# A two-layer hybrid trunk: the mixers' later modulation sums moved from VectorE to TensorE

## The chip, the cores and the metric

One core of one Trainium2 chip runs the whole program. The metric is the device time of one execution in microseconds (us). Three timed runs of the kernel before are shown; the profile is of one further execution. The core's engines work side by side, each through its own queue in order: TensorE (PE: matmuls into PSUM, with PEld for its weight loads), VectorE (DVE), ScalarE (ACT), GpSimd (POOL), and SyncE (SP), which here issues the DMA transfers.

## The reference, cut to what matters

```python
for l in range(DEPTH):                        # 2 layers
    mod = silu(c) @ ada_w[l] + ada_b[l]       # c: 1024 numbers, ada_w[l]: 1024 x 6144
    sh_m, sc_m, g_m, sh_f, sc_f, g_f = split(mod, 6)
    h = rms_norm(x, norm_mix[l]) * (1 + sc_m) + sh_m      # x: 256 x 1024
    proj = h @ w_in[l]
    y_rw, y_ssd, y_fox = three causal mixers on parts of proj
    merged = sum of sigmoid(gate) * (y @ projection)
    x = x + g_m * (merged @ w_out[l])
    h = rms_norm(x, norm_ffn[l]) * (1 + sc_f) + sh_f
    f = dense SwiGLU (l = 0) or top-2-of-8 experts (l = 1)
    x = x + g_f * f
```

The change concerns `mod`, a product of one vector of 1024 numbers and a matrix of 1024 x 6144 in each layer, in float32.

## The kernel before, in words

**Modulations.** A layer's `mod` has six parts of 1024 columns, and each part two halves of 512: 12 halves a layer, 24 in all, each a sum over 1024 rows of `ada_w`. The rows are cut into eight row tiles of 128 x 512, and `silc` holds silu(c) as a column of 128 for each row tile.

The first four halves (scale and shift of the first mixer) are made at the start by `first_half` (L245): eight matmuls whose stationary operand is one column of `silc` broadcast to 32, so that each uses a quarter of TensorE's columns and writes 32 of the 128 PSUM partitions; row tiles 0 to 3 go to quarters 0 to 3, and tiles 4 to 7 are added to them. ACT copies the bank to SBUF with the factor 1/32, and four matmuls of one column with `ones` then sum over partitions and turn the half into columns.

The other 20 halves wait in `mod_queue` and are taken one by one by `mod_next` (L290). Eleven are made during the mixers (layer 0: four, then two; layer 1: four, then one), nine in the first layer's FFN. `mod_load` (L196) issues their transfers on SP:
- where `deep` is not set, four transfers of two row tiles each into `araw`, which has two buffers, so that the third and the fourth transfer wait until the sum has read the first and the second;
- where it is set, eight transfers of one row tile each into the ring `u` of 15 buffers. The sum is then made at the next call.

`mod_sum` (L216) makes the sum on VectorE: one multiply (L220) and seven multiply-adds (L222) of 128 x 512, in the mixers into a tile of the ring `u`, in the FFN into `macc`. `mod_finish` (L225) later turns the result into columns as above.

**The mixers.** Weights come in pieces `raw` of 128 x 2048, are split by ACT (`hi`, L151) and VectorE (`lo`, L152) into two parts, and go through three TensorE products each (`mm3`, L119), with the activations `hh` and `hl` or with a mixer's result. Projections gather in PSUM banks `pd` and `ps` (two buffers each), and the recurrent mixer, the FoX mixer and the modulations use `pm` (four buffers). The recurrent mixer (`rwkv_half`, L525) is a chain of small matmuls, masks (L660, L694) and copies, with matmuls of 32 columns among them.

**Order.** The steps of the mixers are written out by hand in `ORDER`: each word is one step of a generator, and `mo` and `md` are the calls of `mod_next` (the second is the deep one). The framework's scheduler then orders each engine's queue by the order of the program and by its own estimate of when operands are ready; that order is fixed at compile time, so an engine that waits for one instruction's operand holds the rest of its queue. `issue_after` and `behind` put an instruction's queue place behind another's on the same engine. `copied` (L1486, used at L1502) is the copy of the last of the first four halves; ACT's norm work of the column tiles 2 to 7 is placed behind it in both layers.

Of the kernel before, what the change touches and what calls it, by code (L numbers as in the profile page):

```python
# [14 lines left out]
AF = mybir.ActivationFunctionType  # L15
# [4 lines left out]
P = 128  # L20
T = 256
D = 1024
KD = D // P
# [14 lines left out]
NUNIT, NSSD, NSPLIT, NRAW, NB8 = 15, 7, 5, 3, 4  # L38
# [19 lines left out]
def trunk(  # L58
# [5 lines left out]
    pe, act, dve, pool = nc.tensor, nc.scalar, nc.vector, nc.gpsimd  # L64
# [7 lines left out]
    def nm(s):  # L72
        serial[0] += 1
        return f"{s}_{serial[0]}"
# [5 lines left out]
    def const(name, shape, dtype=F32):  # L80
        return cst.tile(shape, dtype, name=name, tag=name)
# [7 lines left out]
    def dbank():  # L89
        return psum.tile([P, 512], F32, name=nm("pd"), tag="pd", bufs=2)  # L90

    def mbank():
        return psum.tile([P, 512], F32, name=nm("pm"), tag="pm", bufs=4)

    def sbank():
        return psum.tile([P, 512], F32, name=nm("ps"), tag="ps", bufs=2)
# [19 lines left out]
    def mm(o, lhsT, rhs, start=True, stop=True):  # L116
        pe.matmul(o, lhsT, rhs, start=start, stop=stop)  # L117
# [49 lines left out]
    def unit(mx, a, b, dtype=F32):  # L167
        return mx("u", [P, a, b], dtype, bufs=NUNIT)
# [10 lines left out]
    silc = const("silc", [P, KD])  # L179
# [8 lines left out]
    def mod_put(l, part, half, ps):  # L188
        o = part * 8 + half * 4
        return dve.tensor_tensor(mods[l][part][:, half * 4:half * 4 + 4], ps, adab[l][:, o:o + 4], op=ALU.add)  # L190
# [3 lines left out]
    mark = {}  # L194
# [19 lines left out]
            mod_sum(sc, raws, key)  # L214

    def mod_sum(sc, raws, key):  # L216
        for kt, raw in enumerate(raws):
            if kt == 0:
                acc = sc("u", [P, 512], bufs=NUNIT) if sc is mx else sc("macc", [P, 512], bufs=3)
                dve.tensor_scalar_mul(acc, raw, silc[:, kt:kt + 1])  # L220
            else:
                dve.scalar_tensor_tensor(acc, raw, silc[:, kt:kt + 1], acc, op0=ALU.mult, op1=ALU.add)  # L222
        mod_late.append((acc, *key))
# [11 lines left out]
    mx = Scope("mix0", stack)  # L235
    FIRST = [(p, h) for p in (1, 0) for h in range(2)]
    araws, last_raw = [], []

    def first_load(n):
# [2 lines left out]
        last_raw.append(nc.sync.dma_start(raw, rows(ada_w[0], (n % 2) * 512, 512, p * D + h * 512, 512)))  # L242
        araws.append(raw)

    def first_half(n):  # L245
        ps = sbank()
        for kg in range(2):
            for q in range(4):
                mm(ps[32 * q:32 * q + 32, :], silc[:, 4 * kg + q:4 * kg + q + 1].broadcast_to([P, 32]), araws[2 * n + kg][:, q, :], kg == 0, kg == 1)
        acc = mx("u", [P, 512], bufs=NUNIT)  # L250
        copied = act.activation(acc, ps, AF.Copy, scale=1.0 / 32)
        ps = dbank()
        for j in range(4):
            mm(ps[:, j:j + 1], acc[:, j * P:(j + 1) * P], ones[:, 0:1])
        mod_put(0, *FIRST[n], ps[:, 0:4])
        return copied

    def make_params(l):
        pp = pcol[:, PCOL + l * NCOL:PCOL + (l + 1) * NCOL]
# [68 lines left out]
    def norm_rows(scr=None, route=False, pieces=4):  # L328

        s8, ss, rs = small(2 * pieces), small(2), small(2)  # L330
        w = D // pieces
        for q in range(pieces):
            for t in range(2):
                if t * w % 512 == 0:
                    sq = sbank()
                o = t * w % 512
                squared = act.activation(sq[:, o:o + w], xr[:, t, q * w:q * w + w], AF.Square, accum_out=s8[:, pieces * t + q:pieces * t + q + 1])
        dve.tensor_reduce(ss, s8.rearrange("p (t q) -> p t q", t=2), AX, ALU.add)
        meant = dve.tensor_scalar(ss, ss, 1.0 / D, EPS, op0=ALU.mult, op1=ALU.add)
        last = rsq(rs, ss)  # L340
        mark.update(root=last, mean=meant, square=squared)
        xt = []
        for k2 in range(KD // 2):
            ps = mbank()
            for k in range(2):
                for t in range(2):
                    transpose(ps[:, k * T + t * P:k * T + (t + 1) * P], xr[:, t, (2 * k2 + k) * P:(2 * k2 + k + 1) * P])
                xt.append(ps[:, k * T:(k + 1) * T])
        if route:
            return xt, rs, last  # L350
        rb = sbank()[:, :T]
        for t in range(2):
            mm(rb[:, t * P:(t + 1) * P], rs[:, t:t + 1].broadcast_to([P, P]), ident)
        rbs = scr()[:, :T]
        act.activation(rbs, rb, AF.Copy)
        return xt, rbs, rs, last

    @contextlib.contextmanager
    def behind(*names):

        with ExitStack() as es:
            for n in names:
                es.enter_context(tc.issue_after(mark[n].ins))
            yield
# [1093 lines left out]
    for lv in range(6):  # L1458
# [8 lines left out]
        ps = mbank()  # L1467
# [15 lines left out]
    first_half(1)  # L1483
    first_half(2)
    normed = norm_rows(lambda: unit(mx, 1, 512)[:, 0, :])
    copied = first_half(3)  # L1486
    last_load = last_raw[7]
    with tc.issue_after(last_raw[7].ins):
        prow = const("prow", [P, 2, 56])
# [3 lines left out]
    for l in range(2):  # L1493
        if l > 0:
            stack = ExitStack()
            mx = Scope("mix1", stack)
        with stack:
            if l > 0:
                normed = norm_rows(lambda: unit(mx, 1, 512)[:, 0, :], pieces=2)
            aff = mod_affine(l, 1, 0, prm["pp"][:, NMIX:NMIX + 8])  # L1500
            norm_cols(aff, normed, 0, 2)
            with tc.issue_after(copied.ins):  # L1502
                norm_cols(aff, normed, 2, KD)
            dump(f"hh{l}", hh)
            run, made = {}, {"y": [None] * 3}
            done = object()

            def part(step):

                i = int(step[1]) if step[1:] in tuple("0123") else 0  # L1510
                if step == "G":
                    made["merged"] = mx("b8", [P, KD, T], bufs=NB8)
                    return gates(mx, l, prm, 0, made["merged"])
                if step[0] == "m":
                    return merge(mx, l, prm, i, made["merged"], made["y"][i], (proj_rw, proj_ssd, proj_fox)[i][l], (4, 8, 4)[i], i == 0)
                return made[step[0]](i)

            def take(step):

                if step == "sc":  # L1520
                    made["key"] = unit(mx, 2, T)
                    made["gl"] = first_cols(l, mx, prm, made["key"])
                    made["r"] = lambda i: rwkv_half(mx, l, prm, made, i)
                elif step == "dt":
                    made["dt"] = logits(mx, made["gl"])
                elif step == "rw":
                    made["y"][0], made["rwkv"] = rwkv(mx, l, prm, lora, made["gl"])
                elif step == "sd":
                    made["y"][1], made["s"] = ssd(mx, l, prm, made["dt"])
                elif step == "fx":  # L1530
                    made["y"][2], made["f"] = fox(mx, l, prm, made["dt"])
                elif step == "mo":
                    mod_next(mx, 0)
                elif step == "md":
                    mod_next(mx, MOD_LEFT[l], True)
                elif step == "gm":
                    while mod_late and mod_late[0][2] == 2:
                        mod_finish(mbank)
                    gm = keep("vfirst", [P, 2, 512]) if l == 1 else mx("u2", [P, 2, 512])
                    made["gm"] = [gm[:, 0], gm[:, 1]]  # L1540
                    mod_row(lambda: unit(mx, 4, P), l, 2, 0.5, made["gm"])
                else:
                    if step not in run:
                        run[step] = part(step)
                    assert run[step] is not None, step
                    if next(run[step], done) is done:
                        run[step] = None
                    return
                assert step in ("mo", "md") or run.setdefault(step, None) is None, step

            with behind("root"):
                take("sc")
            with behind("root"), tc.issue_after(last_load.ins):
                for word in ORDER[l].split()[1:]:
                    name, _, n = word.partition("*")
                    for _ in range(int(n or 1)):
                        take(name)
            assert all(next(g, done) is done for g in run.values() if g)
            merged, gm = made["merged"], made["gm"]
            dump(f"merged{l}", merged)  # L1560
            hh, hl = pair("hh", "hl")
            mod_flush(mx)
            for j in range(0, KD, 2):
                split(merged[:, j:j + 2, :], hh[:, j:j + 2, :], hl[:, j:j + 2, :])
            if l == 0:
                project_out(l, gm, hh, hl)
# [90 lines left out]
```

## Time and profile before

| | us |
|---|---|
| median of three runs | 2163.5 (2162.01 to 2163.97) |
| the profiled execution | 2159.08 |
| its span, first to last instruction | 2157.4 |
| TensorE (PE) busy in the span | 2062.7 |
| VectorE (DVE) busy | 1802.5 |
| ScalarE (ACT) busy | 1383.4 |

The first layer's mixers reach from the start to about 490 us, its FFN from there to about 690, the second layer's mixers to about 1140, and its experts to the end. In the rows below a line number such as L117 is one of the kernel; where a helper issues an operation, as L117 does for all matmuls, the tiles tell them apart: `pd<-hh,hi` writes `pd` from `hh` and `hi`. A count of matmul records is larger than that of the program's instructions where an fp32 product is done in two passes. The chain of waits follows the work that ended last back through the program; its shares say which engine's work, or which transfer, the end waited for.

### The profile page before, as it was taken

The numbers are of one execution on the slowest core, as the hardware profiler recorded it, in microseconds if no ns is written. First come the engines' busy times: TensorE is split into PE (matmuls) and PEld (weight loads), VectorE is DVE, ScalarE is ACT, GpSimd is POOL, SyncE is SP. The second block draws the span as 40 slices with busy tenths as digits, with TensorE's granted clock in tenths as the row PEclk, the third lists the DMA queues.
The fourth block names the chain that finished last, engine by engine and source line by source line (L and its number), as shares of the span: only waits on it lengthen the run. The fifth ranks groups of instructions, "written<-read, shape, count | busy, mean of one in ns | idle before, by whom it ended". The sixth has DMA issues, their size and how long they took to land.

```text
span 2157.4 us, 35317 instructions
## 1 busy us (share of the span) xinstructions
PE 2062.7 (96%) x13291; PEld 1792.2 (83%) x13291; DVE 1802.5 (84%) x2827; ACT 1383.4 (64%) x2198; POOL 146.0 (7%) x184
## 2 busy tenths in 40 slices
PE   6889999999999889999998999999999999999998
PEld 4768799999998878889997888888888887888776
DVE  5877976768776898877678999998999989998887
ACT  3544565555444636556557787878778777877775
POOL 2032300000001032220000000000000000000000
PEclk8999999999999989999999999999999999999999
DMA  8522456557885534426478999999999999999994
GB/s 297 160 75 59 133 183 195 183 181 261 294 281 167 156 100 136 118 87 205 150 230 297 347 371 346 344 353 380 359 331 367 364 356 353 340 343 372 341 354 169
DMA packets 314770, 546.77 MB, mean 253 GB/s; under 512 B 10752, under 2 KB 141952, under 8 KB 314592
## 3 DMA queue, kind: packets, MB, share of 16 engines
q1 hardware_dynamic: 314592, 544.44, 73.2%
q8 instruction: 106, 1.74, 0.3%
q14 instruction: 72, 0.59, 0.1%
HBM read 543.36 MB, written 1.05 MB: 252 GB/s over the span
## 4 chain that ended last, share of the span: by engine, by line
PE 71%; DVE 13%; issue 12%; DMA 2%; ACT 1%; POOL 0%; SPq 0%; DVEq 0%; ACTq 0%; POOLq 0%
PE pd L117 36%; PE pm L117 28%; DVE lo L152 6%; PE ps L117 5%; PE pm L126 1%; DVE u L707 1%; PE ps L126 1%; DVE cu L872 1%; DMA araw<-in_ada_w_dram 1%; DVE xr L1381 1%; DMA prow<-in_heads_dram 1%; ACT hi L151 1%; DVE u L222 0%; DVE dcol L277 0%; DVE lo L433 0%
## 5 line engine op out<-in xcount | busy, mean ns | idle before, releaser
L151 ACT ACTIVATE hi<-raw 128x1024 fp32r<-128x1024 f32 (+2 forms) x1200 | 1026.5, 872 | 507.9 <-PE pd L117 300.4
L152 DVE TENSOR_TENSOR lo<-raw,hi 128x1024 fp32r<-128x1024 f32 (+2 forms) x1200 | 1158.4, 994 | 175.7 <-ACT hi L151 149.7
L117 PE MATMUL pd<-hh,hi 128*128 128x256 f32 (+1 forms) x1184 | 348.6, 296 | 15.9 <-DVE gl L478 3.6
L117 PE MATMUL pd<-hl,hi 128*128 128x256 f32 (+1 forms) x1184 | 342.7, 290 | 0.0
L117 PE MATMUL pd<-hh,lo 128*128 128x256 f32 (+1 forms) x1184 | 342.3, 290 | 0.0
L117 PE MATMUL pm<-lo,hh 128*128 128x512 f32 x672 | 264.8, 395 | 4.5 <-DVE lo L152 4.2
L117 PE MATMUL pm<-hi,hh 128*128 128x512 f32 x672 | 264.6, 394 | 1.1 <-ACT a L1336 1.1
L117 PE MATMUL pm<-hi,hl 128*128 128x512 f32 x672 | 262.0, 390 | 0.0
L117 PEld LDWEIGHTS pd<-hh,hi 128*128 128x128 f32 (+1 forms) x1184 | 232.3, 197 | 28.7 <-issue 10.0
L117 PEld LDWEIGHTS pd<-hl,hi 128*128 128x128 f32 (+1 forms) x1184 | 232.7, 197 | 3.1 <-issue 2.7
L117 PEld LDWEIGHTS pd<-hh,lo 128*128 128x128 f32 (+1 forms) x1184 | 232.2, 196 | 1.8 <-issue 1.2
L117 PE MATMUL pd<-lo,hi 128*128 128x512 f32 x448 | 174.7, 390 | 0.0
L117 PE MATMUL pd<-hi,hi 128*128 128x512 f32 x448 | 170.3, 390 | 0.1
L117 PE MATMUL pd<-hi,lo 128*128 128x512 f32 x448 | 168.2, 390 | 0.0
L117 PEld LDWEIGHTS pm<-lo,hh 128*128 128x128 f32 x672 | 126.2, 188 | 34.9 <-DVE lo L152 9.5
L117 PEld LDWEIGHTS pm<-hi,hh 128*128 128x128 f32 x672 | 126.2, 188 | 28.8 <-ACT a L1336 1.5
L117 PEld LDWEIGHTS pm<-hi,hl 128*128 128x128 f32 x672 | 126.2, 188 | 25.3
L117 PE MATMUL pm<-hi,more 128*128 128x512 f32 x448 | 141.8, 392 | 0.0
L117 PEld LDWEIGHTS pd<-hi,lo 128*128 128x128 f32 x448 | 84.1, 188 | 18.0 <-DVE lo L152 0.2
L117 PEld LDWEIGHTS pd<-hi,hi 128*128 128x128 f32 x448 | 84.1, 188 | 17.9 <-ACT hi L432 0.5
L117 PEld LDWEIGHTS pm<-hi,more 128*128 128x128 f32 x448 | 84.1, 188 | 17.5 <-ACT hi L151 0.3
L117 PEld LDWEIGHTS pd<-lo,hi 128*128 128x128 f32 x448 | 84.1, 188 | 17.3
(436 smaller groups left out, 3394.7 us busy)
## 6 DMA issues: line engine op xcount, KB each, us to landing
raw<-in_moe_w_gu_dram SPq DMA_DIRECT2D x224, 1024.0 KB, 7.0
raw<-in_moe_w_down_dram SPq DMA_DIRECT2D x110, 1024.0 KB, 7.0
raw<-in_w_in_dram SPq DMA_DIRECT2D x66, 1024.0 KB, 5.5
araw<-in_ada_w_dram SPq DMA_DIRECT2D x68, 512.0 KB, 4.9
raw<-in_ffn_w_gu_dram SPq DMA_DIRECT2D x22, 1024.0 KB, 6.6
raw<-in_ffn_w_down_dram SPq DMA_DIRECT2D x11, 1024.0 KB, 6.5
raw<-in_w_in_dram SPq DMA_DIRECT2D x16, 512.0 KB, 5.3
raw<-in_proj_ssd_dram SPq DMA_DIRECT2D x8, 1024.0 KB, 5.7
```

The source lines that it names most:

```text
L117: pe.matmul(o, lhsT, rhs, start=start, stop=stop)
L126: pe.transpose(o, i, ident[:n, :n])
L151: act.activation(hi, raw, AF.Copy)
L152: dve.tensor_sub(lo, raw, hi.bitcast(F32))
L707: dve.transpose(blk(bds[ch], q)[:, odd, bcol(q)], by4(blk(pz, q))[:, odd, :])
L872: dve.scalar_tensor_tensor(cu[:, s:T], ps[:, 0:T - s], pph[:, w:w + 1], cu[:, s:T], op0=ALU.mult, op1=ALU.add)
L1381: dve.tensor_add(xr[:, t, hs], xr[:, t, hs], po)
```

## The change

In the mixers `mod_sum` calls a new function, `quarter_sums`, which makes the sum on TensorE in a `pm` bank, as the first four halves are made in an `ps` bank, and lets ACT copy it into a tile of `u`. The FFN's nine halves stay on VectorE. `first_half` calls the same function. `copied` is no longer handed back; the copy is kept in `mark`, so that in the second layer the place behind it is that of the latest such copy traced.

```diff
     def mod_sum(sc, raws, key):
-        for kt, raw in enumerate(raws):
+        if sc is mx:
+            acc = quarter_sums(mbank(), raws)
+        for kt, raw in enumerate(raws if sc is not mx else ()):
             if kt == 0:
-                acc = sc("u", [P, 512], bufs=NUNIT) if sc is mx else sc("macc", [P, 512], bufs=3)
+                acc = sc("macc", [P, 512], bufs=3)
                 dve.tensor_scalar_mul(acc, raw, silc[:, kt:kt + 1])
             else:
                 dve.scalar_tensor_tensor(acc, raw, silc[:, kt:kt + 1], acc, op0=ALU.mult, op1=ALU.add)
...
+    def quarter_sums(ps, raws):
+
+        for kt in range(KD):
+            q = slice(32 * (kt % 4), 32 * (kt % 4) + 32)
+            mm(ps[q, :], silc[:, kt:kt + 1].broadcast_to([P, 32]), raws[kt], kt < 4, kt >= 4)
+        acc = mx("u", [P, 512], bufs=NUNIT)
+        mark["copied"] = act.activation(acc, ps, AF.Copy, scale=1.0 / 32)
+        return acc
+
     def first_half(n):
-        ps = sbank()
-        for kg in range(2):
-            for q in range(4):
-                mm(ps[32 * q:32 * q + 32, :], silc[:, 4 * kg + q:4 * kg + q + 1].broadcast_to([P, 32]), araws[2 * n + kg][:, q, :], kg == 0, kg == 1)
-        acc = mx("u", [P, 512], bufs=NUNIT)
-        copied = act.activation(acc, ps, AF.Copy, scale=1.0 / 32)
+        acc = quarter_sums(sbank(), [araws[2 * n + kt // 4][:, kt % 4, :] for kt in range(KD)])
         ps = dbank()
         for j in range(4):
             mm(ps[:, j:j + 1], acc[:, j * P:(j + 1) * P], ones[:, 0:1])
         mod_put(0, *FIRST[n], ps[:, 0:4])
-        return copied
...
-            with tc.issue_after(copied.ins):
+            with behind("copied"):
                 norm_cols(aff, normed, 2, KD)
```

## Rows read from the trace of the kernel before

**Rows 1.** The page: busy time, share of the span and instructions of each engine.

```profile
PE 2062.7 (96%) x13291; PEld 1792.2 (83%) x13291; DVE 1802.5 (84%) x2827; ACT 1383.4 (64%) x2198; POOL 146.0 (7%) x184
```

**Rows 2.** Chain of waits by line: 40-100, 250-340, 340-480, 760-860, 960-1060, 1060-1140 us.

```profile
by line: PE pd L117 44.7%; DMA araw<-in_ada_w_dram 11.6%; DVE lo L152 8.0%; DVE cu L872 4.8%; issue 4.5%; ACT hi L151 4.3%; DVE u L222 3.6%; PE pm L117 3.3%; DVE u L605 1.2%; DVE u L615 1.1%; DVE u L616 1.1%; DVE u L606 1.0%; DVE u L609 1.0
by line: PE pd L117 58.2%; PE pm L117 20.3%; PE ps L117 15.5%; PE pm L126 5.4%; PE ps L126 0.6%; issue 0.1%
by line: PE pd L117 78.8%; PE ps L117 11.6%; PE pm L117 7.4%; PE pm L126 2.5%
by line: PE pd L117 27.4%; PE pm L117 11.2%; DMA araw<-in_ada_w_dram 8.9%; DVE lo L152 8.6%; issue 8.3%; DVE u L222 6.2%; DVE u L707 5.2%; PE ps L117 4.3%; DVE s L920 3.2%; DVE b L660 3.1%; PE pm L126 2.7%; DVE cu L872 1.7%; POOL sm L129 1.
by line: PE pd L117 66.8%; PE ps L117 14.4%; PE pm L117 10.9%; PE pm L126 5.4%; ACT hi L151 0.7%; issue 0.6%; ACT b L432 0.6%; ACT u L1015 0.4%; ACT u L1014 0.4%
by line: PE pd L117 78.7%; PE ps L117 14.8%; PE pm L117 4.1%; PE pm L126 2.6%
```

**Rows 3.** Instructions on `silc`: ns min/median/max, first and last start us, forms.

```profile
L222 DVE SCALAR_TENSOR_TENSOR u<-araw,silc,u x56: 732/746/754, 56.2 to 1024.2; 128x512 f32<-128x512 f32 x56
...
L222 DVE SCALAR_TENSOR_TENSOR u<-u,silc,u x21: 740/747/754, 379.3 to 1056.9; 128x512 f32<-128x512 f32 x21
...
L220 DVE TENSOR_SCALAR u<-araw,silc x8: 477/478/484, 55.1 to 1011.4; 128x512 f32<-128x512 f32 x8
L220 DVE TENSOR_SCALAR u<-u,silc x3: 481/482/485, 378.8 to 1046.0; 128x512 f32<-128x512 f32 x3
```

**Rows 4.** First instructions of sums (L220) by stretch: length, VectorE busy (count), clock, DMA.

```profile
40.00:100.00 60.00, 0.48 (x1) 0.96 0.59 176
250.00:480.00 230.00, 2.15 (x5) 1.00 0.60 188
750.00:860.00 110.00, 0.97 (x2) 0.94 0.41 125
950.00:1060.00 110.00, 1.44 (x3) 1.00 0.54 172
```

**Rows 5.** TensorE in order of time, the last of the first four halves.

```profile
28.50 1.06 PE L117 MATMUL ps<-b,silc 128*32 128x512 f32 x8
29.38 1.04 PE L117 MATMUL ps<-raw,silc 128*32 128x512 f32 x8
```

**Rows 6.** TensorE in order of time, around 32-column matmuls of the recurrent mixer.

```profile
142.75 0.28 PE L117 MATMUL pd<-hl,hi 128*128 128x256 f32 x1
142.87 0.28 PE L117 MATMUL pd<-hh,lo 128*128 128x256 f32 x1
143.08 0.64 PE L117 MATMUL pm<-u,c 128*32 128x128 f32 x16
143.65 0.39 PE L117 MATMUL pd<-hh,hi 128*128 128x256 f32 x1
```

**Rows 7.** Waits of the whole span: us in total, times, longest.

```profile
DVE u L222 <- DMA araw<-in_ada_w_dram: 7.0, 9, 1.6
```

**Rows 8.** DMA issues: KB each, median us from issue to landing.

```profile
araw<-in_ada_w_dram SPq DMA_DIRECT2D x68, 512.0 KB, 4.9
```

**Rows 9.** Stretches: length, busy PE, PEld, DVE, ACT, POOL (instructions), clock, DMA.

```profile
55.15:69.20 14.05, 12.64 (x103) 12.38 (x103) 12.45 (x35) 7.70 (x17) 0.00 (x0) 1.00 0.92 274
249.75:266.19 16.44, 16.32 (x150) 14.62 (x149) 16.13 (x34) 11.63 (x33) 3.40 (x2) 1.00 0.53 166
288.12:301.21 13.09, 13.09 (x105) 12.86 (x106) 12.04 (x27) 8.27 (x20) 1.79 (x2) 1.00 0.97 324
750.00:786.00 36.00, 27.42 (x203) 20.96 (x202) 34.13 (x60) 12.41 (x33) 15.17 (x13) 0.87 0.47 137
841.00:857.00 16.00, 15.50 (x118) 13.93 (x117) 14.29 (x31) 7.54 (x17) 5.83 (x5) 1.00 0.68 215
```

**Rows 10.** Instructions of L251, the copy out of PSUM: ns min/median/max.

```profile
L251 ACT ACTIVATE u<-ps x4: 575/588/597, 11.3 to 37.9; 128x512 f32<-128x512 f32 x4
```

**Rows 11.** TensorE's waits in 40 to 250 us: us in total, times, longest.

```profile
PE pm L117 <- DVE u L707: 3.7, 5, 1.3
```

**Rows 12.** The DMA queue's waits in 0 to 490 us: us in total, times, longest.

```profile
SPq L207 <- DVE u L222: 27.5, 12, 8.3
```

More of the change, by code (lines that the diff above doesn't have):

```diff
@@ L1485, in trunk @@
     normed = norm_rows(lambda: unit(mx, 1, 512)[:, 0, :])
-    copied = first_half(3)
+    first_half(3)
     last_load = last_raw[7]
```

## The prediction, made before the change was run

> **What bounds the kernel now.** I read the page's busy shares first, then the chain of waits stretch by stretch, then the rows of the sums themselves. TensorE is busy 96% of the span and VectorE 84% [rows 1]; as averages these decide nothing, so the question is which engine ends last where the sums stand. The chain of waits answers it [rows 2]. In 250 to 480 us, in 960 to 1060 us and after, practically all of it lies on TensorE lines: whatever TensorE gets there makes the kernel longer, and whatever VectorE loses there gives nothing back. In 40 to 100 us and in 760 to 860 us it is mixed: VectorE lines stand in it, among them the sums themselves with the transfers that they wait for ("DMA araw" and "DVE u L222"): 11.6% and 3.6% of 60 us, 8.9% and 6.2% of 100 us, 24.2 us in all.
>
> Eleven of the twenty later modulations are summed in the mixers: the eight first instructions on `araw` and the three on `u` [rows 3]. By stretches, one starts in 40 to 100 us, five in 250 to 480, two in 750 to 860, three in 950 to 1060 [rows 4]. So eight of eleven stand where the chain is all TensorE, and three where VectorE is on it. In the order of the program the mixer of the first layer has four of a first kind (`araw`: two transfers ahead, two asked for during the sum) and then two of a deep kind (`u`: all eight transfers a step ahead), the second layer's four and one. So the eight on the all-TensorE stretches are five of the first kind and three deep ones, and the three on the mixed stretches are of the first kind.
>
> **What goes.** Per modulation one multiply of 0.478 us and seven multiply-adds of 0.746 us [rows 3], 5.70 us of VectorE; 62.7 us for eleven.
>
> **What comes on TensorE.** Eight fp32 matmuls of 32 columns against 128x512, recorded as two passes each. Four of them run at once: in the first four modulations the eight records of one group start within 0.03 us, and the next group starts 0.88 us later, two passes of 0.44 us [rows 5]. What a block of such matmuls costs among full-width ones is seen in the recurrent mixer's 32-column groups: between full-width matmuls 0.12 us apart, a block of 16 records holds the next back until 0.78 us after the last [rows 6]. Less 0.12 and four waves of 128 columns (0.44/4 = 0.11 each) that leaves 0.22 us for changing into column tiles and back. So:
> - a deep modulation, all eight together: 4 x 0.44 + 0.22 = 1.98 us;
> - one of the first kind in two blocks of four: 2 x (0.88 + 0.22) = 2.20 us; in three blocks (four, then two and two, because the third and the fourth transfer land apart): 3.30 us. I take 2.20, because the 32-column groups of the row stand together in TensorE's order and both late transfers can be asked for after one block of 0.9 us; 3.30 stays in the range.
>
> The Trainium skill ("TensorE: Matmul & The Clock Gate", Part 3, measured speedup) gives 3.07 times for four tiles, not four. By that a pass of four would be 0.57 us instead of 0.44, and the eight modulations below would cost 4.2 us more; the next wave's start in the row decides for 0.44.
>
> Where the chain is all TensorE this adds 5 x 2.20 + 3 x 1.98 = 16.9 us, and no row of the chain there shows anything that it could hide behind. If the cover in the other three is missing, they add 2.20 each.
>
> **A wait that moves.** VectorE now waits for `araw` transfers, 7.0 us in 9 times over the eight modulations of the first kind [rows 7], 0.88 us each. A transfer takes 4.9 us from issue to landing in the middle [rows 8]. On VectorE that wait held up `lo` splits, which mostly had room; on TensorE every matmul behind it stands, and so does the next split that waits for its buffers. Bounds for the five: nothing (TensorE has other work ahead of them) to 4.4 us (the same wait). I take half, 2.2.
>
> **What the three on the mixed stretches give back.** Here the engine that is late next is TensorE.
> - 55.15 to 69.20 us: VectorE busy 12.45 of 14.05, TensorE 12.64 [rows 9]. At best the 5.70 of sums and the 1.6 of idle go, 7.3. But TensorE's 12.64 + 2.20 is 14.84, 0.8 more than the stretch. Between +7.3 and -0.8 I take the middle, 3.3.
> - 750 to 786 us: VectorE busy 34.13 of 36.00, TensorE 27.42 [rows 9]. Bounds 0 and 6.4 (36.00 - 27.42 - 2.20). VectorE is 95% busy, so I take 5.0.
> - 841 to 857 us: VectorE 14.29, TensorE 15.50 of 16.00 [rows 9]; 15.50 + 2.20 is 1.7 too long, and VectorE's part is 5.7 at best. Middle: 2.0.
>
> Together 10.3 us.
>
> **Edits at no cost.** The copy out of PSUM, 0.59 us [rows 10], is new on ACT eleven times; ACT is busy 7.7 of 14.05, 8.27 of 13.09 and 11.63 of 16.44 us beside the sums [rows 9], so its idle time hides it; without that cover the eight would add 4.7 us. The sum now holds one of the four `pm` banks from its first matmul to the copy, beside the recurrent mixer, whose matmuls wait at most 1.3 us for the last of their banks' readers [rows 11]; no row shows three banks instead of four; 0 to 3.9 us for the three mixed places, and I take 0. More of the ring `u` stays free, and SyncE's queue, which waits 27.5 us for the sums in the first mixer [rows 12], with weight loads behind it, is let go earlier; I take nothing, because no transfer stands in the all-TensorE chain. The marker for ACT's later norm work is the old one in the first layer, and in the second an instruction long done: 0. The first four modulations issue what they did, and all transfers stay the same in number, size and queue: 0.
>
> **Sum.** 16.9 + 2.2 - 10.3 = +8.8 us. The profiled execution took 2159.08 us (span 2157.4, 1.7 around it); 4.4 below the median of the runs, 2163.5. The sum on its own time is 2167.9; on the median 2172.3. A difference under 0.2%, 4.3 us, can't be told from none here.
>
> **Rivals.**
> - *VectorE's relief decides (faster).* At the three mixed places all 24.2 us of sums and their transfers leave the chain, and the new blocks fall into TensorE's waits there. Then 16.9 - 24.2 = -7.3: 2156.2. For it: VectorE is 95% busy at 750 to 786 us, and SyncE's queue stands behind the sums. Against it: in that stretch other VectorE work runs beside the transfer wait (it idles 1.9 of 36 us), and at 841 us TensorE is as full. It decides once more than 21.2 us leave the chain.
> - *Both cancel (same).* Two thirds of the 24.2 us go, 16.1, and TensorE waits for no transfer: +0.8, 2164.3.
> - *TensorE stands for the late half each time (much slower).* If the second half follows the first at once in TensorE's order, each of the five waits a whole 4.9 us transfer: 24.5 instead of 2.2, +31.1, 2194.6. For it: VectorE's waits for `araw` show that the order runs ahead of the transfers. Against: they are 0.8 us, not 4.9. The Trainium skill ("TensorE: Matmul & The Clock Gate", Part 2, step by step) says that matmuls keep their program order and only weight loads are drawn ahead; by that nothing behind such a wait could pass it.
> - *The tiles don't run together.* If other matmuls are put between the four, each costs 0.88 + 0.22: 8.8 instead of about 2.1 us, eight times: +53.6 on the forecast, 2226. Against it: the groups that stand together [rows 5, 6].
>
> **How the numbers follow.** Forecast 0.46; relief decides 0.22; both cancel 0.24; whole transfer waits 0.05; tiles apart 0.03. Faster 0.22, same 0.24, slower 0.46 + 0.05 + 0.03 = 0.54. The forecast's own range goes from 2167 (waits nothing, a little more given back) to 2186 (three blocks each, 5.5 more; the whole wait, 2.2 more; some 6 of the give-back or of a bank missing). The range takes in the faster case: 2156 to 2186, and leaves out the last two rivals and half of the far ends.
>
> **What would show it.** In the profile after: VectorE's busy time 62 us lower; 176 new fp32 records of 32 columns on `pm`, whose groups of eight start 0.88 us apart; TensorE's chain still whole in 250 to 480 us and that mixer's tail some 11 to 14 us longer from 250 us on; the recurrent stretch at 750 to 786 us about 5 us shorter; small TensorE gaps before the second halves, ended by "DMA araw". Wrong if TensorE's chain at 250 to 480 us turns out to have room for the blocks, or if the two early stretches shorten by over 20 us together.

## The result, and the profile after

The median of three runs is 2224.05 us (2223.91 to 2225.54) against 2163.5, a ratio of 1.0281 [1.0267, 1.0294]: 60.6 us slower. The forecast was 2172 us, 2156 to 2186. The sign was right and the size wrong by 52 us.

The profiled execution of the kernel after took 2223.91 us (span 2222.2). Lines moved down by five: the recurrent mixer's L707 is L712, the copy L251 is L253. The page's busy times, to be held against [rows 1]:

```profile
PE 2125.3 (96%) x13467; PEld 1815.6 (82%) x13467; DVE 1751.7 (79%) x2739; ACT 1390.1 (63%) x2209; POOL 139.7 (6%) x184
```

The 176 new TensorE records are there as forecast, and 88 VectorE instructions are gone. TensorE is busy 62.6 us more, and VectorE 50.8 less, not 62: the 62.7 us of the prediction add up single durations, which overlap in the trace (without the sums VectorE's other work still covers 1751.2 of the 1802.5 us before). The new matmuls, and the engine that stood for the banks of `silc` products (us in total, times):

```profile
L117 PE MATMUL pm<-araw,silc x128: 592/604/1064, 56.0 to 1081.5; 128*32 128x512 f32 x128
...
L117 PE MATMUL pm<-u,silc x48: 592/592/617, 400.6 to 1118.1; 128*32 128x512 f32 x48
...
who waited for it (us, times):
  ACT u L253: 28.4, 11
```

The chain of waits of the kernel after, in the stretches that answer to [rows 2] (now 41 to 103, 259 to 363, 363 to 515, 795 to 901 and 1000 to 1123 us):

```profile
by line: PE pd L117 65.1%; PE pm L117 8.4%; DVE lo L152 4.4%; DVE cu L877 3.4%; issue 3.0%; PE ps L117 1.5%; DVE u L610 1.2%; DVE u L620 1.1%; DVE u L621 1.1%; PE pm L126 1.0%; ACT hi L151 1.0%; DVE u L580 1.0%; DVE u L611 1.0%; DVE u L616 
by line: PE pd L117 46.9%; PE pm L117 24.3%; PE ps L117 11.3%; DMA raw<-in_w_in_dram 5.1%; PE pm L126 3.7%; DVE lo L152 2.5%; DVE u L712 1.7%; issue 1.0%; ACT hi L151 0.8%; DVE s L897 0.7%; ACT u L253 0.6%; DVE b L438 0.6%; ACT u L724 0.5%;
by line: PE pd L117 68.0%; PE pm L117 13.5%; PE ps L117 10.5%; DMA raw<-in_proj_fox_dram 3.2%; PE pm L126 2.4%; DVE lo L152 0.9%; ACT hi L151 0.9%; issue 0.5%; ACT gt L1055 0.3%; ACTq L151 0.0%; DVE b L1089 0.0%
by line: PE pd L117 33.5%; PE pm L117 23.9%; PE ps L117 6.1%; DMA araw<-in_ada_w_dram 5.6%; DVE lo L152 5.6%; DVE u L712 5.5%; issue 4.1%; PE pm L126 2.6%; DVE cu L877 2.2%; DVE s L945 1.5%; DVE s L925 1.1%; DVE c L720 0.9%; DVE xb L880 0.8
by line: PE pd L117 54.1%; PE pm L117 22.4%; PE ps L117 12.0%; PE pm L126 5.6%; DMA araw<-in_ada_w_dram 3.1%; ACT u L253 1.0%; ACT u L797 0.6%; ACT u L992 0.5%; issue 0.4%; ACT u L785 0.3%; ACTq L797 0.0%; ACTq L785 0.0%; ACTq L253 0.0%
```

In 40 to 100 us the sums and `DMA araw` have left the chain, as the prediction wanted, and TensorE's lines have filled the place. In the stretches where TensorE was practically the whole chain it isn't any more: weight transfers, `lo`, ACT's copies and the late halves stand in it.

Now the blocks in order of time (start, us, instruction; in brackets idle time and what ended it). First one deep modulation whole, then the first of the next deep one, then the modulation at 1009 us:

```profile
400.48 0.22 PE L117 MATMUL pm<-nmq,identb 128*128 128x128 bf16 x1
400.63 1.92 PE L117 MATMUL pm<-u,silc 128*32 128x512 f32 x16
402.48 0.39 PE L117 MATMUL pd<-b,lo 128*128 128x256 f32 x1
...
407.96 0.28 PE L117 MATMUL pd<-b,lo 128*128 128x256 f32 x1
408.17 1.04 PE L117 MATMUL pm<-u,silc 128*32 128x512 f32 x2
409.14 0.51 PE L117 MATMUL pd<-b,hi 128*128 128x256 f32 x2
409.49 0.28 PE L117 MATMUL pd<-b,lo 128*128 128x256 f32 x1
409.60 0.40 PE L117 MATMUL pd<-b,hi 128*128 128x256 f32 x2
409.93 1.04 PE L117 MATMUL pm<-u,silc 128*32 128x512 f32 x2
...
1009.33 1.06 PE L117 MATMUL pm<-araw,silc 128*32 128x512 f32 x8
1014.23 3.24 PE L117 MATMUL pm<-araw,silc 128*32 128x512 f32 x8 [3.83 <-DMA araw<-in_ada_w_dram]
1018.50 0.39 PE L117 MATMUL pd<-hi,hh 128*128 128x256 f32 x1 [1.03 <-ACT u L992]
```

Eight matmuls side by side (16 records) hold TensorE back 2.0 us. Where the order put another product between each two of them, one matmul alone costs 1.18 from the start before it to the next one's start, 1.06 above the usual 0.12, and the modulation 8.5. I call this the time that a block takes: last start before it to first start behind it, less the pitch that the instruction before has otherwise. Over the eleven modulations of the kernel after it is 45.7 us, in 31 blocks: 3 of eight matmuls, 8 of four, 12 of two, 8 of one.

### The profile page after: what moved, and what is told of

Its sections match the earlier page's. It is cut to its first block, busy times and chain, and to the rows that moved or that the text cites. A ratio compares the mean times of both kernels' runs of the same rounds, so it can differ in the third digit from the quotient of the medians.

```text
span 2222.2 us, 35556 instructions
## 1 busy us (share of the span) xinstructions
PE 2125.3 (96%) x13467; PEld 1815.6 (82%) x13467; DVE 1751.7 (79%) x2739; ACT 1390.1 (63%) x2209; POOL 139.7 (6%) x184
## 3 DMA queue, kind: packets, MB, share of 16 engines
HBM read 543.36 MB, written 1.05 MB: 245 GB/s over the span
## 4 chain that ended last, share of the span: by engine, by line
PE 72%; DVE 12%; issue 12%; ACT 2%; DMA 2%; POOL 0%; SPq 0%; DVEq 0%; ACTq 0%; POOLq 0%
PE pd L117 35%; PE pm L117 30%; DVE lo L152 5%; PE ps L117 5%; PE pm L126 1%; DVE u L712 1%; PE ps L126 1%; ACT hi L151 1%; DVE cu L877 1%; DVE xr L1386 1%; DMA prow<-in_heads_dram 1%; DMA araw<-in_ada_w_dram 0%; DVE dcol L282 0%; DVE lo L438 0%; DVE a L1342 0%
```

## The experiments

Each is an edit of the kernel after; differences are against the kernel before, run on the same chip. Kernels that leave work out say so in what was expected.

**Is VectorE's relief worth anything?** `e1_none` makes no sums at all:

```diff
-            acc = quarter_sums(mbank(), raws)
+            acc = mx("u", [P, 512], bufs=NUNIT)
+            act.activation(acc, raws[0], AF.Copy, scale=1.0 / 32)
```

> Leaves out the sums of the mixers' eleven modulations on both engines: ACT copies one row tile in their place, the transfers stay. Theory A (TensorE's own time for the blocks, and what waits with it, is the cost; VectorE's relief is worth nothing): as before, 2163 +-6, so that the change's 60 us are all from TensorE's blocks. Rival B (VectorE's relief is worth its share of the chain, 24 us, but the new order of the queues lost more): 2140 to 2150. If it comes out well above 2170, the order alone, made new at compile time, costs that much.

Measured 2163.48 us, ratio 1.0004 [0.9994, 1.0014]. With VectorE's eleven sums gone and next to nothing in their place, the time stays. So the eleven together give nothing back; that one place gains and another loses as much is not ruled out.

**Which modulations cost?** The sum is on TensorE for chosen keys only, and on VectorE as before for the others:

```diff
-        if sc is mx:
+        here = sc is mx and key in ((0, 2, 0),)                         # e2_first
+        here = sc is mx and key in ((0, 3, 0), (0, 3, 1), (1, 5, 1))    # e3_deep
+        here = sc is mx and key in ((0, 2, 0), (1, 4, 1), (1, 3, 0))    # e6_three
+        if here:
             acc = quarter_sums(mbank(), raws)
```

> Only the first of the eleven (that at 55 us) on TensorE, the other ten on VectorE as before. A: +2 to +3 us, the two blocks, and nothing later: about 2166. Rival B (one moved sum lays TensorE's queue anew, and the recurrent stretch at 150 to 240 us becomes longer, as it did by 7 us in the changed kernel where no sum stands): +8 to +12, about 2173, with the shift standing from 240 us on.

Measured 2167.83 us (ten runs, 2161.45 to 2171.44), ratio 1.0022 [1.0011, 1.0033]: +4.3, between the two forecasts and nearer to A. The two blocks took 3.3 us. The profiled execution (2171.28) does have rival B's longer recurrent stretch, which comes back below with the clock.

> Only the three deep modulations on TensorE, the eight of the first kind on VectorE as before. A: the blocks' own time, 3 x 2.0 us if whole, 2.0 + 8.5 + 2.0 if the second is cut into eight pairs as in the changed kernel: +6 to +13, 2169 to 2176. B: more than 20 us over, 2184 or more, spread over places without a block.

Measured 2179.68, ratio 1.0078 [1.0061, 1.0095]; +16.1, some 4 us above A's range. Of it the blocks took 12.5: 2.0, eight times about 1.06, and 1.95.

> Only the three modulations of the mixed stretches (the ones at 55, 759 and 842 us) on TensorE, the other eight on VectorE as before. The prediction gave these three 10.3 us back in all, so 2153 to 2158 us beside a median of 2163.6. Theory A (VectorE's relief is worth nothing at any of them, TensorE's blocks add their own time): three times 2.2 to 3.3 us and the waits for the late halves: 2170 to 2176 us.

Measured 2186.37 (2183.30 to 2192.60), ratio 1.0110 [1.0089, 1.0130]. Both numbers missed: the blocks took only 9.5 us of the +22.3. These were the three places that were to give 10.3 back.

**Do the late halves cost?** `e4_early` reads the first four row tiles twice, so that no sum waits for a late transfer (ten modulations are then one block; the second deep one is still cut, into four):

```diff
-            acc = quarter_sums(mbank(), raws)
+            acc = quarter_sums(mbank(), raws[:4] * 2)
```

> As the changed kernel, but row tiles 4 to 7 are taken from the first two transfers (the late two are still made and not read): no sum waits for a late transfer. This computes other sums. A: eleven whole groups of 2.0 us, 22 us on TensorE instead of 45.7, and no stall: about 2188 to 2195. Rival C (the late transfer and the cut blocks cost little; the time goes in the order of the rest): 2210 or more.

Measured 2190.49, ratio 1.0118 [1.0099, 1.0136]: +26.9, and the blocks took 25.8. More than half of the 60.6 us hangs on the late halves and on how they are cut.

**Cut or wait?** `e5_whole` takes the same row tiles in another order (the deep modulations backwards, the others 0 to 3, then 6, 7, 4, 5), so that the tile that comes last is asked for first and the rest of its group stands with it:

```diff
-        for kt in range(KD):
+        for n, kt in enumerate(order):
             q = slice(32 * (kt % 4), 32 * (kt % 4) + 32)
-            mm(ps[q, :], ..., raws[kt], kt < 4, kt >= 4)
+            mm(ps[q, :], ..., raws[kt], n < 4, n >= 4)
```

> The order of the row tiles alone is changed: the deep modulations go through them from the last to the first, those of the first kind take the last transfer's tiles before the third's. In the order of TensorE's queue each deep one is then one block of eight and each of the first kind two blocks of four, and no deep one is cut in eight. Theory 1 (what the late halves cost beyond the eleven whole groups, some 34 us, is the cutting into small blocks, each with its own change of tiles): TensorE's own time in the blocks falls from 45.7 to about 24 to 26 us, and the time to 2190 to 2205 us. Theory 2 (it is the wait of TensorE for the late halves and of ACT's copy behind them, whatever the blocks' size): 2215 us or more, with TensorE waits for DMA araw of some us each, because nothing of a half can start before its last transfer. In between: both.

Measured 2200.62 (2192.25 to 2208.07), ratio 1.0171 [1.0137, 1.0205]: 24 us of the 60.6 are gone by order alone. The blocks took 33.6 us, not 24 to 26, because TensorE still stands for the late half of one modulation (5.25 us, and then passes at a granted clock of 0.50). The trace of this kernel, a deep one and that one:

```profile
404.61 0.28 PE L117 MATMUL pd<-hh,hi 128*128 128x256 f32 x1
404.81 1.92 PE L117 MATMUL pm<-u,silc 128*32 128x512 f32 x16
406.67 0.39 PE L117 MATMUL pd<-ysh,hi 128*128 128x256 f32 x1
...
981.20 1.06 PE L117 MATMUL pm<-araw,silc 128*32 128x512 f32 x8
987.51 1.94 PE L117 MATMUL pm<-araw,silc 128*32 128x512 f32 x8 [5.25 <-DMA araw<-in_ada_w_dram]
990.52 0.58 PE L117 MATMUL pd<-hi,hh 128*128 128x256 f32 x1 [1.08 <-ACT u L992]
```

`e9_nostall` leaves that one on VectorE:

```diff
+        here = sc is mx and key != (1, 3, 1)
```

> The kernel with the row tiles taken in the other order, but the one modulation at whose second half TensorE stood for a late transfer (981 us, 9.4 us in all) is summed on VectorE as before. Theory 1 (TensorE's own time in the blocks is the cost, the waits included): 9 to 12 us below that kernel's 2200.6, 2187 to 2192 us. Rival (the wait only takes the place of other waits there): 2198 us or more.

Measured 2193.96 (2188.60 to 2197.62), ratio 1.0145 [1.0127, 1.0164]: +30.2 instead of +36.5, and the number missed by 2 us. The blocks took 24.4 us, 9.2 less. The runs of the two kernels overlap (2188.60 to 2197.62 and 2192.25 to 2208.07): that the wait costs time at the end is likely, but they don't show it.

**ACT's copies.** `e7_dvecopy` puts the eleven copies on VectorE:

```diff
-        mark["copied"] = act.activation(acc, ps, AF.Copy, scale=1.0 / 32)
+        if late:                                  # the eleven, not the first four
+            dve.tensor_scalar_mul(acc, ps, 1.0 / 32)
+        else:
+            mark["copied"] = act.activation(acc, ps, AF.Copy, scale=1.0 / 32)
```

> As after, but the copy of the eleven sums out of PSUM stands on VectorE instead of ACT. In after these copies wait 28.4 us at the head of ACT's queue. If that wait holds back ACT's hi splits and through them TensorE, 2195 to 2212 us. If the cost is TensorE's own (blocks and its waits), nothing changes or it is a little worse, because VectorE now waits in ACT's place: 2218 to 2232 us.

Measured 2218.93, ratio 1.0258 [1.0241, 1.0275]: 54.9 us over before instead of 60.6, hardly clear of noise, since the two intervals overlap. The blocks took 43.4 us, 2.3 less. The 28.4 us of the expectation were misread: they hold the first four halves too. ACT's waits in the kernel after (us, times, longest):

```profile
ACT u L253 <- PE pm L117: 16.1, 9, 9.1
...
ACT u L253 <- PE ps L117: 12.3, 2, 7.6
```

Only the first row is the change's. TensorE pays for part of it: behind the blocks at 1014 and 1081 us it stood 1.03 and 0.97 us for copies of ACT (L992) that come behind the sum's in ACT's queue.

**Columns or change of tiles?** `e8_thin` keeps the program's order and lets the matmuls of the eleven sums read 16 columns (`w`); the rest of each sum is set to zero by GpSimd, and ACT copies 16 columns. Its trace has 34 blocks instead of 31:

```diff
-            mm(ps[q, :], ..., raws[kt], kt < 4, kt >= 4)
+            mm(ps[q, :w], ..., raws[kt][:, :w], kt < 4, kt >= 4)
```

> As after, but the matmuls of the eleven sums read 16 of 512 columns (the other 496 columns of each sum are left out and set to zero by GpSimd); blocks, their cuts, their waits for transfers and the order stay. If the cost is the matmuls' columns (about 0.43 us a wave of four, 2 waves a pass): the blocks fall from 45.7 us to some 8 to 12 (31 blocks at 0.22 to 0.35 us), and the time to 2180 to 2195 us. If it is waits for transfers and ACT and the order that they force: 2205 us or more.

Measured 2194.45, ratio 1.0142 [1.0125, 1.0159]: inside the first range. The blocks took 11.6 us instead of 45.7, and the time fell 29.6. So the columns, with ACT's longer copies, are half of the loss. A single of this kernel:

```profile
401.09 0.28 PE L117 MATMUL pd<-b,lo 128*128 128x256 f32 x1
401.30 0.23 PE L117 MATMUL pm<-u,silc 128*32 128x16 f32 x2
401.47 0.51 PE L117 MATMUL pd<-b,hi 128*128 128x256 f32 x2
```

From 401.09 to 401.47 is 0.38, 0.26 over the usual 0.12, with next to no columns in it: that I take for the change into column tiles and back, the 0.22 that the prediction read from [rows 6].

**The prediction's terms one by one**, with the order of `e5_whole` (the times in the expectations are those of its trace or of the kernel after):

```diff
+        here = sc is mx and key in ((0, 3, 0), (0, 3, 1), (1, 5, 1))               # e10_deepwhole
+        here = sc is mx and key in ((0, 2, 1), (0, 4, 0), (0, 4, 1), (1, 5, 0))    # e11_four
+        here = sc is mx and key == (1, 4, 1)                                       # e12_one759
```

> Only the three deep modulations on TensorE, each as one block of eight in its order. The prediction's term for them: 3 x 1.98 = 5.9 us, 2168.5 to 2171 us beside a median of 2163.6 to 2164.1, against 2179.7 where the second of them was cut into eight single blocks. If the cut is not the cause of that 16.1 us: 2176 us or more.

Measured 2168.02 (twelve runs), ratio 1.0019 [1.0006, 1.0033], +4.3; the blocks took 5.89 us, the forecast 5.94. Beside `e3_deep` this shows what the cut of one modulation into eight costs: 11.8 us, of which 6.6 are in blocks.

> Only four modulations of the first kind in the all-TensorE stretches (254, 297, 326 and 1045 us) on TensorE, each in two blocks of four. The prediction's term: 4 x 2.20 = 8.8, with half of VectorE's transfer waits 1.8 more: 2172 to 2175 us. If late halves or ACT's copies cost more than the blocks: 2180 us or more. No block stands ahead of the recurrent stretch of the first mixer, so I expect its granted clock to be that of before.

Measured 2184.37 (2178.17 to 2188.65), ratio 1.0093 [1.0070, 1.0116], +20.6: the rival's number. The blocks took 10.5 us. Six of the eight took 1.05 to 1.09 each, and two late ones 1.90 and 2.12, as here (the kernel's TensorE):

```profile
260.92 0.28 PE L117 MATMUL ps<-hi,hl 128*128 128x256 f32 x1
261.13 1.06 PE L117 MATMUL pm<-araw,silc 128*32 128x512 f32 x8
262.94 0.45 PE L117 MATMUL pm<-u,b 128*64 128x64 f32 x4 [0.74 <-ACT u L254]
```

The next matmul stands for ACT's copy (L254) out of the sum's bank. The clock of the first recurrent stretch did not fall (0.98 in 140 to 215 us, 0.94 before). In 250 to 340 us this kernel's chain, all TensorE in [rows 2], has other engines again:

```profile
by line: PE pd L117 50.3%; PE pm L117 24.3%; PE ps L117 10.8%; PE pm L126 3.3%; DVE lo L152 2.7%; DVE u L713 2.0%; ACT hi L151 1.5%; issue 1.1%; DVE s L898 0.8%; DVE sm L1001 0.8%; ACT u L254 0.7%; DVE b L439 0.7%; ACT u L725 0.6%; ACT b L1
```

> Only the modulation at 759 us on TensorE, in two blocks of four: the place where VectorE is 95% busy. The prediction gave back 5.0 us there: 2158 to 2160 us. Theory A (the relief is worth nothing, the blocks add 2.2): 2165 to 2168 us. If the granted clock of the recurrent stretches falls with it, as in the kernel with three: up to 2176 us.

Measured 2167.62 (twelve runs), ratio 1.0018 [1.0008, 1.0027], +3.9. The kernel's program stands 6.3 us behind at 750, so the same work has to be found first, by the columns that TensorE's matmuls have worked off, the block's own left out. The work of 750 to 795 and of 795 to 880 us of the kernel before, there and in `e12_one759` (columns as in [rows 9]):

```profile
750.00:795.00 45.00, 36.42 (x266) 29.63 (x264) 40.95 (x77) 16.29 (x41) 15.17 (x13) 0.85 0.40 118
795.00:880.00 85.00, 82.08 (x779) 73.44 (x780) 70.58 (x164) 52.50 (x131) 14.55 (x18) 1.00 0.42 125
```

```profile
756.30:796.80 40.50, 37.00 (x275) 29.15 (x274) 31.69 (x68) 17.48 (x42) 12.61 (x13) 0.92 0.44 131
796.80:890.60 93.80, 85.95 (x787) 75.81 (x787) 71.32 (x165) 53.58 (x130) 14.14 (x18) 0.96 0.38 112
```

So the stretch itself did become shorter, 40.5 us with the block in it, and 39.4 in `e1_none`, against 42.9 to 45.0 in the five traces that keep the sum on VectorE there (before, `e2_first`, `e3_deep`, `e10_deepwhole`, `e11_four`). But the work behind it then took 93.8 and 90.6 us, at a granted clock of 0.96 and 0.94, against 84.9 to 89.4 at 0.98 to 1.00. By 880 us the gain was gone. (In the kernel after, which has three blocks there, the stretch took 46.0.) Each is one execution; why the work behind takes longer stays open.

## Where the rest went: the granted clock

Blocks of 45.7 us leave 14.9 of the 60.6 over, and in `e6_three` 12.8 of 22.3. Some of it is more cutting, of matmuls that the change does not touch. The recurrent mixer's `pm<-u,u` uses half of TensorE's rows (64*128). Around 900 us of the kernel before, four groups of eight records stand whole; in the kernel after, `e6_three`, `e4_early` and `e7_dvecopy` the new order cuts them into seven or eight groups, and a group of four records takes as long as one of eight (before, then after):

```profile
898.01 0.28 PE L117 MATMUL pd<-hh,lo 128*128 128x256 f32 x1
898.22 1.14 PE L117 MATMUL pm<-u,u 64*128 64x256 f32 x8
899.29 0.39 PE L117 MATMUL pd<-hh,hi 128*128 128x256 f32 x1
```

```profile
934.52 0.28 PE L117 MATMUL pd<-hl,hi 128*128 128x256 f32 x1
934.73 1.13 PE L117 MATMUL pm<-u,u 64*128 64x256 f32 x4
935.78 0.39 PE L117 MATMUL pd<-hh,lo 128*128 128x256 f32 x1
```

From the start before a group to the start behind it, the four took 5.1 us and the seven of the kernel after 10.0, one of them at half clock. No run holds this cut alone.

For the rest, look at 140 to 215 us, the first layer's recurrent stretch, which holds no block in any kernel (rows in four fences: before; `e10_deepwhole`; after; `e12_one759`; length, busy PE, PEld, DVE, ACT, POOL with instructions, clock, DMA):

```profile
140.00:215.00 75.00, 68.92 (x613) 60.23 (x612) 51.54 (x121) 35.20 (x86) 14.52 (x22) 0.94 0.25 71
```

```profile
140.00:215.00 75.00, 66.42 (x611) 57.90 (x615) 51.17 (x122) 35.20 (x88) 13.47 (x20) 0.98 0.25 71
```

```profile
140.00:215.00 75.00, 67.35 (x569) 59.27 (x569) 48.13 (x116) 34.87 (x88) 10.30 (x18) 0.86 0.24 69
```

```profile
140.00:215.00 75.00, 68.19 (x569) 59.68 (x567) 47.74 (x111) 33.99 (x84) 11.27 (x18) 0.88 0.23 65
```

At a granted clock of 0.94 to 0.98 of 2.4 GHz TensorE gets through 611 to 613 records, at 0.86 to 0.88, with more of the stretch at 1.2 GHz, 569. In the kernel after, 7% fewer. The modulation at 55 us, ahead of it, is a suspect: all eight kernels that have it on TensorE show 0.86 to 0.89 here, and of the six that don't five show 0.94 to 0.98. `e2_first`, which moves no other, also ran at a lower clock as a whole (median 0.977 of ten runs, before 0.980 of nineteen beside them). But it isn't needed: `e12_one759`, the last row, is the sixth. It has no block before 759 us, its instructions up to there stand on TensorE, VectorE, ACT and GpSimd in the order of the kernel before, and its profiled execution still has the lower clock here. So the same instructions run this stretch at either clock, from one execution to the next; that the modulation at 55 us, or the order that comes with it, makes the lower one likelier is suggested by these runs and not shown.

An account over the whole run: (1 - mean granted clock) x span, median of a kernel's runs, is what TensorE's clock takes at most, 43.3 us before (49 runs) and 57.8 after.

| kernel | us over before | taken in blocks | clock, over before's 43.3 | left |
|---|---|---|---|---|
| e1_none | -0.1 | 0 | 1.0 | -1.1 |
| e12_one759 | 3.9 | 2.2 | 0.0 | 1.7 |
| e2_first | 4.3 | 3.3 | 6.6 | -5.6 |
| e10_deepwhole | 4.3 | 5.9 | 1.1 | -2.7 |
| e3_deep | 16.1 | 12.5 | 1.3 | 2.3 |
| e11_four | 20.6 | 10.5 | 6.9 | 3.2 |
| e6_three | 22.3 | 9.5 | 12.4 | 0.4 |
| e4_early | 26.9 | 25.8 | 2.7 | -1.6 |
| e9_nostall | 30.2 | 24.4 | 7.2 | -1.4 |
| e8_thin | 30.4 | 11.6 | 13.7 | 5.1 |
| e5_whole | 36.5 | 33.6 | 8.4 | -5.5 |
| e7_dvecopy | 54.9 | 43.4 | 7.7 | 3.8 |
| after | 60.6 | 45.7 | 14.5 | 0.4 |

The two terms give every kernel's loss within 6 us (also when `e9_nostall` to `e12_one759` are held against the 23 runs before beside them alone, which adds 2.2 us to their clock). The first is measured in one profile of each, and `e4_early`, `e5_whole`, `e8_thin` and `e10_deepwhole` moved it on purpose. The second is an account, not an experiment: no kernel changed the clock alone, a slow clock costs nothing where TensorE waits anyway, a block at half clock counts in both terms, and the cut of `pm<-u,u` has no term of its own. What sets the clock of such a stretch, and why all three runs of the kernel after are at the low end (0.973 to 0.974 over the run; before, 0.975 to 0.984 in 49 runs), stays open; so does why the parts don't add (the modulations at 55 and 759 us cost 3.3 and 2.2 in blocks and about 4 each alone, and with the one at 842 us 22.3).

## Why the prediction was wrong

- **The sums on all-TensorE stretches, 16.9 us: mis-sized, 36.5 in the trace.** The unit was right: 0.22 for the change of tiles (0.26 with 16 columns), 0.44 a wave, three whole deep ones 5.89 against 5.94. The failed step is "the 32-column groups of the row stand together in TensorE's order". That was read from groups that wait for no transfer [rows 5, 6]; here the scheduler laid products between matmuls whose operands come by different transfers. (The eight records of a group there start in two fours, 0.45 us apart, not all within 0.03 us; the price of 0.88 stays.) Six of the eight modulations of the first kind have three blocks (3.2 to 4.2 us instead of 2.20) and one deep one has eight (8.5 instead of 1.98). The order of row tiles alone takes 24 us off (`e5_whole`).
- **The wait that moves, 2.2 us: right in kind, wrong in size and spread.** Almost all of it is one modulation, 3.83 us of waiting, then passes at a granted clock of 0.58 and 1.03 us for ACT: 9.2 us with its matmuls, which the 36.5 above hold already. What it costs in the end stays within noise (6.3 us, `e9_nostall` against `e5_whole`). The rival "TensorE stands for the late half each time" was true once in eight.
- **The give-back, -10.3 us: failed.** It is 0 for all eleven together (`e1_none`), and at the surest place +3.9 where -5.0 stood (`e12_one759`). The stretch there did become shorter; the failed step is that this shortens the whole. VectorE's place in the chain of one stretch did not tell what the work behind it would take. The three places add their blocks too, 9.2 us.
- **Edits at no cost.** ACT's copy was put at 0. Its place in ACT's queue isn't free: TensorE stood 1.03 and 0.97 us for what comes behind it and once 0.70 for the copy itself, which holds a `pm` bank until then; with the copy on VectorE the blocks took 2.3 us less (`e7_dvecopy`).
- **Missing from the sum:** the clock, up to 14.5 us by the account above, and the cut of the mixer's own groups, 4.9 us of which some is clock.
- **The rival "the tiles don't run together"** gave 2226, close to the time by chance. Its mechanism holds for one modulation of eleven; all others run at least two tiles side by side.

So 16.9 + 2.2 - 10.3 should have read 45.7 in blocks with their waits, nothing back, and up to 14.5 of clock.

## What to carry to other kernels

Before pricing column-tiled matmuls, ask what a scheduler will put between them: a group costs one change of tiles and one wave per pass only while its members are neighbours, and operands that land apart split it. Look at the groups that the change does not touch, too: the new order cut some of them. Before counting on relief, take the work out and time that: a kernel without it says about what any other place for it can give. And a change's account should name the granted clock beside the work: here the two together gave every kernel's time within 6 us, and either alone did not.

## What the runs showed of the hardware

- Changing into column tiles and back costs 0.26 us even when the tile does next to nothing (0.38 against 0.12 between neighbours in `e8_thin`). The Trainium skill ("TensorEngine Tiling (Array Packing)", Tiling Modes, Key Properties) says that changing the tiling mode drains TensorE, without a price; the trace fits that and gives one.
- Less its change of tiles, the deep modulation in eight singles took 8.5 - 8 x 0.22 = 6.7 us, and the whole one 2.0 - 0.22 = 1.8: some 3.8 times for four tiles. The 3.07 that the prediction quoted from the Trainium skill ("TensorE: Matmul & The Clock Gate", Part 3, measured speedup) stands there for four row tiles; these four fp32 column tiles do better.
- One and the same program varies with its clock: of `e10_deepwhole`'s twelve runs the one at 0.985 took 2161.95 us and the one at 0.975 2173.87, though not strictly in step (the slowest, 2174.00, ran at 0.979), while the three runs of the kernel after lie within 1.6 us.
